# Two layers of a three-mixer decoder trunk: the up projection's three products per step as two, and the gated features on GpSimd

## The chip, the core and the metric

The kernel runs on one core of a Trainium2 chip. The metric is the device time of one execution in microseconds, as the median of the runs. The engines are TensorE (PE in the rows; its weight loads are PEld), VectorE (DVE), ScalarE (ACT), GpSimd (POOL) and SyncE (SP), which issues most transfers. SBUF is the working memory, PSUM (banks of 128 x 512 float32) takes TensorE's results; GpSimd has no access to PSUM.

## What is computed

Two layers over 256 positions of 1024 features, float32. The part that the change touches is the feed-forward half of each layer, cut from the reference:

```python
h = rmsnorm(x, norm_ffn)
u = causal_depthwise_conv(h @ w_up, conv_w, conv_b)     # w_up: 1024 x 5632, 3 taps
u_a, u_v = jnp.split(u, 2, axis=-1)                     # 2816 features each
return x + (jax.nn.silu(u_a) * u_v) @ w_down            # w_down: 2816 x 1024
```

Ahead of it each layer has one combined input projection, three attention-like mixers and their merge. The output is a final rmsnorm.

## The kernel before

**Products in two parts.** Float32 numbers are cut into a high part (a copy rounded to TensorE's 32-bit format F32R) and a low part (the number minus the high part). A product is then three: high weights x high activations, high x low, low x high (`three`, L347). Activations lie with the position as the free axis, 256 columns, with the two halves of the positions interleaved by `turns` when TensorE reads them.

**Weights.** `weights` (L260) loads a piece of 1 MB by a transfer on SP into one of 4 `raw` tiles, ScalarE writes the high part `whi` (L271), VectorE the low part `wlo` (L272): in this text a "split". One piece makes two pairs of 128x1024, and there are 6 buffers of each (`wp`), so TensorE must be done with a pair before the pair six later can be written. A pair serves 8 k steps of one 128-wide block of output features, called a tile below: 24 products.

**Up projection** (L733 to L782). Eleven passes `i`, each with two pieces (`a` = 0 for the features that go through silu, 1 for the others) of two tiles `f`: four tiles a pass. A tile's result has 256 columns in a PSUM tile (`at` for a = 0, `mm` for a = 1, `at` for both in the last pass; four banks each). `conv` (L719) does the convolution: ScalarE's Identity with the last tap as scale and the bias (L727), then two steps of VectorE, `scalar_tensor_tensor` shifted by one and by two positions (L728, L729). In the first pass the row scale of the norm isn't known yet, and VectorE multiplies it in (L724). Then silu on ScalarE (L768), the product with the other half on VectorE (L770), and a split of the result into `gT`, again by L271 and L272. All small tiles come from a pool `quarter` of 8 buffers.

**Down projection.** In layer 0 (L783 to L795) each of 8 output blocks runs over all k = 0 to 21 before the next begins, 22 x 3 products of 256 columns; `grow` adds the result to x. In layer 1 (L798 on) four sums run side by side over k = 0 to 17, and over k = 18 to 21 at the end, with products of 512 columns. There passes 4 to 7 of the up projection also transpose a piece of x, and ScalarE copies it (L782).

**Order.** TensorE's program order is as written. A scheduler places the instructions of VectorE, ScalarE and GpSimd in their queues when the program is built; each engine then takes its queue in order and waits at its head. GpSimd has little to do before: the power of the norm (L309, L821) and one multiply of 128x512 in `scaled` (L336).

Of the kernel before, what the change touches and what calls it, by code (L numbers as in the profile page):

```python
# [9 lines left out]
F32 = mybir.dt.float32  # L10
F32R = mybir.dt.float32r
BF = mybir.dt.bfloat16
AF = mybir.ActivationFunctionType
OP = mybir.AluOpType
# [4 lines left out]
S = 256  # L19
# [98 lines left out]
def trunk(ctx: ExitStack, tc: tile.TileContext, x, wpack, vecs, sinks, gain_out, rope, masks, fc, out):  # L118
    nc = tc.nc
# [11 lines left out]
    f3 = lambda a, n=S: a.rearrange("p (k n) -> p k n", n=n)  # L131

    def mm(n=512):
        t = pm.tile([128, 512], F32, name="mm", tag="mm")
        return t
# [13 lines left out]
    def parts(mov, k):  # L149

        return mov[k // 2][:, k % 2] if isinstance(mov, list) else mov[:, k]

    def turns(v):

        return (v if len(v.shape) == 3 else v.rearrange("p (h i) -> p h i", h=2)).rearrange("p h i -> p i h")
# [5 lines left out]
    def halves(v):  # L161
        return v.rearrange("p (h i) -> p h i", h=2) if len(v.shape) == 2 else v.rearrange("p a (h i) -> p a h i", h=2)
# [5 lines left out]
    def quarter():  # L168
        return tp.tile([128, S], F32, name="quarter", tag="quarter", bufs=8)
# [6 lines left out]
    def matmul(out, lhsT, rhs, **kw):  # L176
        n = 1
        for k in rhs.shape[1:]:
            n *= k
        clock[0] += n / 2400 * (4 if lhsT.dtype == F32 else 1)  # L180
        return nc.tensor.matmul(out, lhsT, rhs, **kw)  # L181
# [9 lines left out]
    def resume(task):  # L191
        try:
            task[0] = next(task[1]) + clock[0]
        except StopIteration as e:
            tasks.remove(task)
            task[1] = None

    def tick():
        for task in list(tasks):
            if clock[0] >= task[0]:  # L200
                resume(task)
                break
# [11 lines left out]
    first = [rawp.tile([128, 2048], F32, name="raw", tag="raw") for _ in range(2)]  # L214
# [45 lines left out]
    def weights(l, i, n=1024):  # L260

        r = rawp.tile([128, 2048], F32, name="raw", tag="raw")
        nc.sync.dma_start(r, wpack[l, i])
        w = [new_cut() for _ in range(2)]
        for a in range(0, 2048, n):
            hi, lo = (q[:, a % 1024 : a % 1024 + n] for q in w[a // 1024])
            split(hi, lo, r[:, a : a + n])
        return lambda a, n: [q[:, a % 1024 : a % 1024 + n] for q in w[a // 1024]]

    def split(hi, lo, src):  # L270
        a = nc.scalar.activation(hi, src, AF.Copy)  # L271
        return a, nc.vector.tensor_tensor(lo, src, hi.bitcast(F32), OP.subtract)  # L272
# [74 lines left out]
    def three(ps, lh, ll, rh, rl, first, last):  # L347
        ps, rh, rl = ps.rearrange("p (i h) -> p i h", h=2), turns(rh), turns(rl)
        matmul(ps, lh, rh, start=first, stop=False)
        matmul(ps, lh, rl, start=False, stop=False)  # L350
        matmul(ps, ll, rh, start=False, stop=last)
        tick()

    def gemm_a(l, i, act, n=512):

        ws = [weights(l, i)] + ([weights(l, i + 1)] if n == 512 else [])
        per = 2048 // n
        ps = [mm(), mm()]
        for t, k in [(t, k) for k in range(8) for t in range(2)]:
            wh, wl = ws[k // per](k % per * n, n)  # L360
            three(ps[t][:, :n], act[:, k, t, 0, :], act[:, k, t, 1, :], wh, wl, k == 0, k == 7)
        return ps

    def gemm_b(w, f, mov, ps, nk=8, ks=None):

        for k in ks or range(nk):
            wh, wl = w((f * nk + k) * 128, 128)
            v = parts(mov, k)
            three(ps, wh, wl, v[:, :, 0, :], v[:, :, 1, :], k == 0, k == nk - 1)

    def rotary(dst, ps, t, nh, kind):

# [180 lines left out]
    last = DEPTH - 1  # L553

    ctx.enter_context(tc.manual_schedule(engines={mybir.EngineType.PE}))
    for l in range(DEPTH):
        pc = 0
        vB = f3(blk(), 512)
        if l == 0:
            st = {}  # L560
            ps = [mm(), mm()]
            for k in range(KT):
# [5 lines left out]
                if k % 2 == 0:  # L568
                    wh, wl = new_cut()
# [8 lines left out]
        else:  # L578
            ps = gemm_a(l, pc, st["h"])
        h = st["h"]  # L580
# [4 lines left out]
        for n in range(2):  # L585
            d = f3(blk())
            for c in range(2):
                w = ahead if l == 0 and pc == 2 else weights(l, pc)
                pc += 1
                ps = [(at if n == 0 and c == 1 else mm)() for _ in range(2)]  # L590
# [19 lines left out]
        h = scaled(2 * l, rb)  # L610
# [32 lines left out]
        for n in range(2):  # L643
            ps = gemm_a(l, pc, h)
            pc += 2
            tr.append(spawn(rotated(qkC[n], ps, 8, 2 * n)))
        ps = gemm_a(l, pc, h)
# [6 lines left out]
        ps = gemm_a(l, pc, h)  # L654
# [4 lines left out]
        ps = gemm_a(l, pc, h, n=256)  # L659
# [10 lines left out]
        for hf in range(2):  # L670
            m, mp = blk(), [blk2() for _ in range(2)]
            for i in BRANCHES:
                sg = blk()
                for c in range(2):
                    w = weights(l, pc)
                    pc += 1
                    for f in range(2):
                        p = mm()
                        gemm_b(w, f, h, p[:, :S])
                        j = 2 * c + f  # L680
# [3 lines left out]
                w = weights(l, pc)  # L684
                pc += 1
                until("ABC"[i])
                for f in range(4):
                    p = mm()
# [14 lines left out]
        for fs in ((0, 1, 2, 3), (4, 5), (6, 7)):  # L703
            w = [weights(l, pc + i) for i in range(len(fs) // 2)]
            pc += len(w)
            ps = [mm() for _ in fs]
            for r in range(2):
                for f, p in zip(fs, ps):
                    for k in range(4 * r, 4 * r + 4):
                        wh, wl = w[(f - fs[0]) // 2]((f % 2 * 8 + k) * 128, 128)  # L710
                        v = parts(mg, k)
# [4 lines left out]
        h = st["h"]  # L716
        tn = spawn(norm_scales(st, NORM[1]))
        gT = []
        def conv(ps, a, i):  # L719
            for f in range(2):  # L720
                j, p = a * NF + 2 * i + f, ps[f]
                if i == 0:
                    q = quarter()
                    nc.vector.tensor_tensor(q, p[:, :S], rb, OP.mult)  # L724
                    p = q
                u = quarter()
                nc.scalar.activation(u, p[:, :S], AF.Identity, scale=col(l, 88 + j), bias=col(l, 132 + j))  # L727
                nc.vector.scalar_tensor_tensor(u[:, 1:S], p[:, 0 : S - 1], col(l, 44 + j), u[:, 1:S], op0=OP.mult, op1=OP.add)  # L728
                nc.vector.scalar_tensor_tensor(u[:, 2:S], p[:, 0 : S - 2], col(l, j), u[:, 2:S], op0=OP.mult, op1=OP.add)  # L729
                us.append(u)  # L730

        ahead = None
        for i in range(11):  # L733
            us, pend = [], []
            if i == 1:
                h = hs
            for a in range(2):
                w = ahead or weights(l, pc, n=1024 if i else 512)
                ahead = None
                pc += 1  # L740
                ps = [(at if a == 0 or i == 10 else mm)() for _ in range(2)]
                if i == 0 and a == 0:
                    gemm_b(w, 0, h, ps[0][:, :S], ks=range(7))
                    gemm_b(w, 1, h, ps[1][:, :S], ks=range(7))
                    for f in range(2):
                        gemm_b(w, f, h, ps[f][:, :S], ks=[7])
                    finish(tn)
                    rb = st["row"]
                    hs = scaled(2 * l + 1, rb)
                else:  # L750
                    for f in range(2):
                        gemm_b(w, f, h, ps[f][:, :S])
                if i == 0:
                    pend.append((ps, a))
                    if a == 0:
                        continue
                else:
                    pend = [(ps, a)]
                if i == 0 and a:
                    ahead = weights(l, pc)  # L760
                for ps, a in pend:
                    conv(ps, a, i)
            for f in range(2):
                k = 2 * i + f
                if k % 2 == 0:
                    gT.append(blk2())
                sa = quarter()
                last_silu = nc.scalar.activation(sa, us[f], AF.Silu)  # L768
                g = quarter()
                nc.vector.tensor_tensor(g, sa, us[2 + f], OP.mult)  # L770
                split(*(parts(gT, k)[:, :, j, :] for j in range(2)), halves(g))
            if l == last and i == 3:

                xe = np_.tile([128, 4096], F32, name="xe", tag="xg")
                xn, gB = f3(xe[:, : 2 * D], D), xe[:, 2 * D : 3 * D]
                nc.sync.dma_start(gB, bass.AP(tensor=gain_out.tensor, offset=gain_out.offset, ap=[[0, 128], [1, D]]))
            if l == last and 4 <= i < 8:
                t, c = divmod(i - 4, 2)
                p = mm()
                for j in range(4):  # L780
                    transpose(p[:, j * 128 : j * 128 + 128], xT[:, 4 * c + j, t * 128 : t * 128 + 128])
                nc.scalar.activation(xn[:, t, c * 512 : c * 512 + 512], p, AF.Copy)  # L782
        if l < last:  # L783
            st = {}
            for f in range(KT):
                p = mm()
                for k in range(NF):
                    j = f * NF + k
                    if j % 16 == 0:
                        w = weights(l, pc)  # L790
                        pc += 1
                    wh, wl = w((j % 16) * 128, 128)
                    v = parts(gT, k)
# [4 lines left out]
    ps = [[mm(), mm()] for _ in range(2)]  # L798
# [4 lines left out]
    for t, c, k in order:  # L803
        wh, wl = ws[k // 2]((k % 2) * 1024 + c * 512, 512)
# [3 lines left out]
        if c == 0:  # L808
            y = blk()
            ss = sp_.tile([128, 2], F32, name="ss", tag="ss")  # L810
            v = sp_.tile([128, 1], F32, name="v", tag="v")
# [49 lines left out]
```

## Time and profile before

| | |
|---|---|
| median of 3 runs | 838.12 us (836.96 to 838.51) |
| profiled execution | 837.95 us, span 836.2 |
| busy TensorE, VectorE, ScalarE, GpSimd | 822.5, 654.6, 536.9, 15.2 us |
| up projection of layer 0, passes 2 to 10 | 265.5 to 361.8 us of the span |

The span is what the engines show, the rest lies around it. Busy time of TensorE is modelled and overlaps itself, so the distance from one product's start to the next is the better measure of what one costs. A row of the timeline has start, length, engine, line, operation, tiles (written <- read), shapes, and in brackets the idle time before it and what ended it; rows of the same kind in succession are merged, with their count.

### The profile page before, as it was taken

Reading aid. Unit: us, or ns where it says so; the run is one execution under the profiler, and the core shown is the slowest. Engines: PE = TensorE matmul, PEld = TensorE weight load, DVE = VectorE, ACT = ScalarE, POOL = GpSimd, SP = SyncE. Lnnn points to the kernel's source line nnn. Section 1 sums busy time; section 2 is a strip of 40 time slices with the busy share of each in tenths; the row PEclk is TensorE's granted clock in tenths of the full one; section 3 lists DMA queues with packets and bytes.
Section 4 is the critical chain, followed back from the end, with each engine's and each line's share of the span. In section 5 each row is a group of like instructions: output and inputs, shape, how many; then the busy total and the mean of one; then the engine's idle time right before and its main releaser. Section 6 shows DMA issues by size and latency. Waiting matters only on the chain.

```text
span 836.2 us, 16477 instructions
## 1 busy us (share of the span) xinstructions
PE 822.5 (98%) x6710; PEld 784.4 (94%) x6710; DVE 654.6 (78%) x1225; ACT 536.9 (64%) x893; POOL 15.2 (2%) x17
## 2 busy tenths in 40 slices
PE   8899999999999999999999999999999999999996
PEld 6888899999999999999999889999999999999885
DVE  6878798776689998876658878896568899888543
ACT  7576478665568776664446766686556687666442
POOL 0100000000010000000000000000000100000000
PEclk9999999999999999999999999999999999999998
DMA  9654442555554665565655432545664467555511
GB/s 348 261 196 151 152 146 91 206 193 182 193 202 151 213 217 192 193 200 198 201 201 198 151 107 100 201 152 158 203 199 163 162 214 249 194 202 196 203 55 50
DMA packets 22635, 151.49 MB, mean 181 GB/s; under 512 B 2656, under 2 KB 3168, under 8 KB 4896
## 3 DMA queue, kind: packets, MB, share of 16 engines
q1 hardware_dynamic: 21744, 148.86, 51.7%
q8 instruction: 52, 0.85, 0.4%
q10 hardware_dynamic: 576, 0.80, 0.3%
q0 software_dynamic: 240, 0.79, 0.3%
q14 instruction: 23, 0.19, 0.1%
HBM read 149.39 MB, written 1.05 MB: 180 GB/s over the span
## 4 chain that ended last, share of the span: by engine, by line
PE 91%; issue 4%; DVE 3%; ACT 2%; POOL 1%; POOLq 0%; ACTq 0%
PE mm L181 67%; PE at L181 21%; PE at L185 2%; DVE half L343 1%; DVE wlo L272 1%; ACT whi L271 0%; POOL rn L309 0%; PE at L316 0%; DVE hs L272 0%; ACT half L457 0%; ACT half L456 0%; ACT half L455 0%; POOL gx L217 0%; PE mm L185 0%; DVE half L459 0%
## 5 line engine op out<-in xcount | busy, mean ns | idle before, releaser
L272 DVE TENSOR_TENSOR wlo<-raw,whi 128x1024 fp32r<-128x1024 f32 (+1 forms) x292 | 342.8, 1180 | 115.2 <-ACT whi L271 115.0
L271 ACT ACTIVATE whi<-raw 128x1024 fp32r<-128x1024 f32 (+1 forms) x292 | 296.4, 1022 | 190.5 <-PE mm L181 155.6
L181 PE MATMUL mm<-hs,whi 128*128 128x256 f32 x1344 | 229.1, 276 | 0.0
L181 PEld LDWEIGHTS mm<-hs,whi 128*128 128x128 f32 x1344 | 204.1, 192 | 1.0 <-issue 0.8
L181 PE MATMUL mm<-hs,wlo 128*128 128x256 f32 x672 | 184.8, 275 | 0.0
L181 PE MATMUL mm<-blk,whi 128*128 128x256 f32 x992 | 168.1, 276 | 0.0
L181 PEld LDWEIGHTS mm<-blk,whi 128*128 128x128 f32 x992 | 150.6, 192 | 0.6 <-issue 0.3
L181 PE MATMUL mm<-blk,wlo 128*128 128x256 f32 x496 | 136.4, 275 | 0.0
L181 PEld LDWEIGHTS mm<-hs,wlo 128*128 128x128 f32 x672 | 129.0, 192 | 0.0
L181 PE MATMUL at<-hs,whi 128*128 128x256 f32 x704 | 120.1, 276 | 1.5 <-DVE hs L272 1.5
L181 PEld LDWEIGHTS at<-hs,whi 128*128 128x128 f32 x704 | 107.2, 192 | 1.9 <-DVE hs L272 1.8
L181 PE MATMUL at<-hs,wlo 128*128 128x256 f32 x352 | 96.8, 275 | 0.0
L181 PEld LDWEIGHTS mm<-blk,wlo 128*128 128x128 f32 x496 | 95.2, 192 | 0.0
L181 PE MATMUL mm<-whi,hs 128*128 128x512 f32 (+1 forms) x320 | 93.3, 364 | 0.0
L181 PEld LDWEIGHTS at<-hs,wlo 128*128 128x128 f32 x352 | 67.6, 192 | 0.0
L181 PEld LDWEIGHTS mm<-whi,hs 128*128 128x128 f32 x320 | 58.4, 189 | 8.0 <-issue 0.3
L181 PE MATMUL mm<-wlo,hs 128*128 128x512 f32 (+1 forms) x160 | 57.3, 358 | 0.0
L181 PE MATMUL mm<-whi,blk 128*128 128x512 f32 x176 | 52.5, 379 | 0.0
L181 PE MATMUL mm<-xg,whi 128*128 128x256 f32 x256 | 43.3, 276 | 0.0
L181 PEld LDWEIGHTS mm<-xg,whi 128*128 128x128 f32 x256 | 39.0, 192 | 0.1
L181 PEld LDWEIGHTS mm<-whi,blk 128*128 128x128 f32 x176 | 33.3, 189 | 4.7
L523 ACT ACTIVATE blk<-blk,nm 128x128 f32<-128x128 f32 (+1 forms) x64 | 28.2, 443 | 13.4 <-DVE nm L520 13.3
(125 smaller groups left out, 1057.6 us busy)
## 6 DMA issues: line engine op xcount, KB each, us to landing
raw<-in_wpack SPq DMA_DIRECT2D x138, 1024.0 KB, 5.0
raw<-in_wpack SPq DMA_DIRECT2D x3, 512.0 KB, 8.9
gx<-in_x POOLq DMA_DIRECT2D x3, 256.0 KB, 7.3
raw<-in_wpack SPq DMA_DIRECT2D x2, 256.0 KB, 4.7
xe<-in_gain_out SPq DMA_DIRECT2D x1, 512.0 KB, 3.5
out<-blk SPq DMA_DIRECT2D x2, 256.0 KB, 2.1
out<-blk ACTq DMA_DIRECT2D x2, 256.0 KB, 2.5
mkt<-in_masks SPq DMA_DIRECT2D x1, 320.0 KB, 7.6
```

The costliest lines, as they stand in the source:

```text
L181: return nc.tensor.matmul(out, lhsT, rhs, **kw)
L185: nc.tensor.transpose(out, in_, ident)
L271: a = nc.scalar.activation(hi, src, AF.Copy)
L272: return a, nc.vector.tensor_tensor(lo, src, hi.bitcast(F32), OP.subtract)
L343: nc.vector.scalar_tensor_tensor(n[:, k], order(xT[:, 2 * c + k, :]), gain(gi, 2 * c + k), rp, op0=OP.mult, op1=OP.mult)
L523: nc.scalar.activation(e[:, i * w : i * w + w], e[:, i * w : i * w + w], AF.Exp, bias=nm[:, j : j + 1], accum_out=sm[:, j : j + 1])
```

## The change

In passes 2 to 10 (`i > 1`) of both layers the high weights meet both parts of the activations in one product of 512 columns, whose two halves of a PSUM bank are added afterwards; the low weights are added onto the first half. ScalarE copies the second half to SBUF, VectorE adds it to the first, and the convolution reads that sum. In all passes the gated product and its low part are computed by GpSimd, the product in place. Line numbers of the changed kernel are 8 to 18 higher.

```diff
+    def two(ps, lh, ll, v, first, last):
+        both = v.rearrange("p h j i -> p (j i) h")
+        matmul(f3(ps, 2), lh, both, start=first, stop=False)
+        matmul(f3(ps[:, :S], 2), ll, turns(v[:, :, 0, :]), start=False, stop=last)
+        tick()
...
             v = parts(mov, k)
-            three(ps, wh, wl, v[:, :, 0, :], v[:, :, 1, :], k == 0, k == nk - 1)
+            if ps.shape[-1] == 2 * S:
+                two(ps, wh, wl, v, k == 0, k == nk - 1)
+            else:
+                three(ps, wh, wl, v[:, :, 0, :], v[:, :, 1, :], k == 0, k == nk - 1)
...
+                elif i > 1:
+                    q = quarter()
+                    nc.scalar.activation(q, p[:, S:], AF.Copy)
+                    nc.vector.tensor_tensor(q, p[:, :S], q, OP.add)
+                    p = q
...
-                        gemm_b(w, f, h, ps[f][:, :S])
+                        gemm_b(w, f, h, ps[f] if i > 1 else ps[f][:, :S])
...
-                g = quarter()
-                nc.vector.tensor_tensor(g, sa, us[2 + f], OP.mult)
-                split(*(parts(gT, k)[:, :, j, :] for j in range(2)), halves(g))
+                g = sa
+                nc.gpsimd.tensor_tensor(g, sa, us[2 + f], OP.mult)
+                hi, lo = (parts(gT, k)[:, :, j, :] for j in range(2))
+                nc.scalar.activation(hi, halves(g), AF.Copy)
+                nc.gpsimd.tensor_tensor(lo, halves(g), hi.bitcast(F32), OP.subtract)
```

VectorE's queue in a settled pass of layer 0 before, from the gated product of one pass on (L770, then two `blk` rows for its low part; `wlo` is a split, L728 and L729 the convolution):

```order
L770 TENSOR_TENSOR quarter<-quarter 128x256
L272 TENSOR_TENSOR wlo<-raw,whi 128x1024
L272 TENSOR_TENSOR blk<-quarter,blk 128x2x128 x2
L728 SCALAR_TENSOR_TENSOR quarter<-at,vec,quarter 128x255
L729 SCALAR_TENSOR_TENSOR quarter<-at,vec,quarter 128x254
L272 TENSOR_TENSOR wlo<-raw,whi 128x1024
```

The same engine in a settled pass after (L740 is the addition of the halves, L744 and L745 the convolution):

```order
L272 TENSOR_TENSOR wlo<-raw,whi 128x1024
L744 SCALAR_TENSOR_TENSOR quarter<-quarter,vec 128x255
L740 TENSOR_TENSOR quarter<-mm,quarter 128x256
L745 SCALAR_TENSOR_TENSOR quarter<-quarter,vec 128x254
L272 TENSOR_TENSOR wlo<-raw,whi 128x1024
```

The gated product and its low part are gone from the queue, and an addition stands in each tile's stretch between the two convolution steps of the tile before; one split stands beside one tile's convolution in both.

ScalarE at the end of layer 0's up projection after (L739 copies the second half, L743 is the Identity, L784 silu, L788 the high part of the gated product, which reads what GpSimd wrote; L624 loads the table of the next layer's functions):

```order
L739 ACTIVATE quarter<-at 128x256
L271 ACTIVATE whi<-raw 128x1024
L743 ACTIVATE quarter<-quarter,vec 128x256
L739 ACTIVATE quarter<-at 128x256
L271 ACTIVATE whi<-raw 128x1024
L743 ACTIVATE quarter<-quarter,vec 128x256
L784 ACTIVATE quarter<-quarter 128x256 x2
L624 ACT_TABLE_LOAD
L788 ACTIVATE blk<-quarter 128x2x128 x2
L271 ACTIVATE whi<-raw 128x1024 x2
```

And before, at the same place (L727 the Identity, L768 silu, `blk` the high part):

```order
L727 ACTIVATE quarter<-at,vec 128x256
L271 ACTIVATE whi<-raw 128x1024
L727 ACTIVATE quarter<-at,vec 128x256
L768 ACTIVATE quarter<-quarter 128x256 x2
L271 ACTIVATE whi<-raw 128x1024
L271 ACTIVATE blk<-quarter 128x2x128 x2
L613 ACT_TABLE_LOAD
L271 ACTIVATE whi<-raw 128x1024
L285 ACTIVATE xg<-gx 128x2x128
```

A copy now stands ahead of every tile's weight split, and the last two high parts stand behind the table load and ahead of the next weight splits.

## Rows read from the trace of the kernel before

**Rows 1.** The page's first part: busy us, share of the span, instructions.

```profile
PE 822.5 (98%) x6710; PEld 784.4 (94%) x6710; DVE 654.6 (78%) x1225; ACT 536.9 (64%) x893; POOL 15.2 (2%) x17
```

**Rows 2.** Chain of waits in order of time: start us, us, what.

```profile
286.92 5.36 PE at L181 x48
...
772.40 51.82 PE mm L181 x240
```

**Rows 3.** Windows, up projection of layer 0: length; PE, PEld, DVE, ACT, POOL; clock.

```profile
274.70:285.40 10.70, 10.70 (x98) 10.70 (x97) 10.70 (x20) 7.71 (x14) 0.00 (x0) 1.00 0.65 215
...
306.80:317.50 10.70, 10.70 (x98) 10.70 (x98) 9.54 (x17) 7.32 (x13) 0.00 (x0) 1.00 0.58 194
```

**Rows 4.** Waits from 306.8 to 349.6: us in total, times, longest.

```profile
ACT whi L271 <- PE mm L181: 9.3, 8, 1.2
ACT whi L271 <- PE at L181: 4.2, 8, 0.6
```

**Rows 5.** Timeline: a split on VectorE, and the first product of pass 2.

```profile
261.06 1.22 DVE L272 TENSOR_TENSOR wlo<-raw,whi 128x1024 fp32r<-128x1024 f32 x1
...
265.31 0.39 PE L181 MATMUL at<-hs,whi 128*128 128x256 f32 x2
```

**Rows 6.** Operations on `quarter` tiles: line, engine, count; ns min/median/max; first and last start.

```profile
L768 ACT ACTIVATE quarter<-quarter x44: 399/405/422, 262.8 to 774.0; 128x256 f32<-128x256 f32 x44
L770 DVE TENSOR_TENSOR quarter<-quarter x44: 412/423/443, 264.1 to 775.9; 128x256 f32<-128x256 f32 x44
L727 ACT ACTIVATE quarter<-at,vec x44: 536/547/562, 265.6 to 773.3; 128x256 f32<-128x256 f32 x44
L728 DVE SCALAR_TENSOR_TENSOR quarter<-at,vec,quarter x44: 475/479/499, 267.7 to 774.6; 128x255 f32<-128x255 f32 x44
L695 DVE TENSOR_TENSOR quarter<-mm,blk x32: 412/417/425, 149.6 to 629.9; 128x256 f32<-128x256 f32 x32
L727 ACT ACTIVATE quarter<-quarter,vec x8: 583/600/612, 255.3 to 669.5; 128x256 f32<-128x256 f32 x8
L728 DVE SCALAR_TENSOR_TENSOR quarter<-quarter,vec x8: 477/480/484, 256.5 to 670.9; 128x255 f32<-128x255 f32 x8
```

**Rows 7.** GpSimd: groups by line (count, busy us, mean ns), and timeline.

```profile
L821 POOL TENSOR_TENSOR r<-v,mhalf 128x1 f32<-128x1 f32 x2 | 1.1, 550 | 170.6 <-DVE v L819 170.6
L852 POOL MEMSET const-bfloat16-1.0<- 128x1 bf16 x1 | 0.1, 101 | 0.0
...
29.74 1.28 POOL L336 TENSOR_TENSOR half<-gx,rb 128x512 f32<-128x512 f32 x1 [1.30 <-DVE rb L319]
...
657.62 2.33 POOL L336 TENSOR_TENSOR half<-gx,rb 128x512 f32<-128x512 f32 x1 [1.40 <-DVE rb L319]
```

**Rows 8.** Timeline of VectorE beside those two instructions.

```profile
30.37 0.41 DVE L604 SCALAR_TENSOR_TENSOR blk<-at,rb 128x256 f32<-128x256 f32 x1
...
657.36 1.22 DVE L272 TENSOR_TENSOR wlo<-raw,whi 128x1024 fp32r<-128x1024 f32 x1
658.50 1.76 DVE L343 SCALAR_TENSOR_TENSOR half<-gx,rb 128x256 f32<-128x256 f32 x1
...
662.05 0.93 DVE L343 SCALAR_TENSOR_TENSOR half<-gx,rb 128x256 f32<-128x256 f32 x2
```

**Rows 9.** End of layer 0's up projection: VectorE's timeline; the down projection's first products.

```profile
366.90 0.76 DVE L272 TENSOR_TENSOR blk<-quarter,blk 128x256 fp32r<-128x256 f32 x2
...
L181 PE MATMUL mm<-blk,whi x139: 275/275/275, 361.8 to 384.9; 128*128 128x256 f32 x139
```

**Rows 10.** Windows at the start of the program, columns as in rows 3.

```profile
24.40:28.40 4.00, 1.88 (x16) 1.69 (x16) 3.46 (x4) 0.52 (x1) 2.72 (x1) 1.00 1.01 416
...
29.75:33.16 3.41, 3.41 (x19) 3.41 (x18) 3.34 (x8) 1.43 (x2) 1.27 (x1) 0.50 1.01 423
```

**Rows 11.** ScalarE's copies of the transposed x in layer 1, columns as in rows 6.

```profile
L782 ACT ACTIVATE xe<-mm x4: 584/586/589, 708.0 to 741.4; 128x512 f32<-128x512 f32 x4
```

## The prediction

> **What bounds the kernel now.** I read the page's busy times first, then the chain of waits through the up projections, then a table of windows over that stage, and last single rows of VectorE (DVE) and GpSimd (POOL). TensorE (PE) is busy 98% of the span, VectorE 78% [rows 1]. In the up projection the chain is TensorE alone: every run of 48 products of 256 columns takes 5.36 us, so one product costs 5.36/48 = 0.1117 us and the three of one k step 0.335 us [rows 2]. I call the 8 k steps of one 128-wide block of w_up a tile: 2.68 us. One pass of the loop over `i` has four tiles, 10.72 us.
>
> VectorE is close behind. In a settled pass (306.8 to 317.5) it works 9.54 of 10.70 us, ScalarE (ACT) 7.32; at 274.7 to 285.4 VectorE is busy all the time [rows 3]. What gives it room is a lead. There are six buffers of weight halves, so the split of tile c+6 may begin when tile c is done; in the settled stretch ScalarE waits for TensorE before it can split on, 9.3 + 4.2 us in 42.8, which is the sign of a full lead [rows 4]. At the first pass that the change touches (i = 2) the lead is small: the low halves of its first tile are ready at 261.06 + 1.22 = 262.28, and TensorE uses them at 265.31, 3.0 us later [rows 5].
>
> **The change, part by part.** TensorE: 9 passes x 4 tiles x 8 k steps x 2 layers = 576 steps lose one of three products and get the same columns in two. 512 columns cost 51.82/240 = 0.2159 us in the down projection of layer 1 [rows 2]. A step becomes 0.2159 + 0.1117 = 0.3276 instead of 0.3350: 7.4 ns less, 4.2 us in all, a tile 2.62 us, a pass 10.48. The upper end of the cost is no gain (the pair as long as three products), the lower one no overhead left (768 columns at 0.2159/512 = 0.3239, 6.4 us less). I take 4.2, since the row with 512 columns has the same 32-bit operands read with the same turn.
> The rows show 5 ns of a 256-column product beyond its share at 2.4 GHz (256/2.4 = 106.7 ns), and 2.6 ns of a 512-column one (213.3). The Trainium skill, TensorE: Matmul & The Clock Gate, section "Wait — 56ns, not 53.3ns?", has one fixed cost of about 2.5 ns for every product, whatever its width; by that rule the merge would give only 576 x 2.5 ns = 1.4 us (an estimate) where the rows give 4.2.
>
> VectorE: a pass loses two multiplies and two subtractions of 128x256 (0.42 each) and gets four additions with one input in PSUM; the nearest row, L695, takes 0.417. Its two convolution steps read an SBUF tile in place of PSUM, 0.48 either way [rows 6]. So its own work stays 9.54 a pass.
> ScalarE: four copies more, between 0.405 (SBUF, L768) and 0.547 (PSUM, L727), and the Identity from SBUF 0.600 in place of 0.547 [rows 6]: 1.8 to 2.4 a pass on 7.32, so 9.1 to 9.7 of 10.48. That hides behind TensorE as long as ScalarE doesn't wait.
> Buffers: 10 `quarter` tiles a pass in place of 8, in 8 buffers; a copy then waits for a tile of the pass before, which costs nothing while GpSimd is done within a pass. PSUM banks come free earlier, at the addition. The weight DMAs keep their order on SP.
>
> GpSimd is where I see the cost: four instructions a pass, each with SBUF inputs. The trace has one such operation in this program, L336, 128x512: 1.28 us alone [rows 7]. At 657.62 it finds VectorE in a split of two SBUF inputs (657.36 to 658.58) and takes 2.33: it waited 0.96 and then ran about as long as alone. VectorE's next instruction, also of two SBUF inputs, is issued at 658.50 and takes 1.76, where the two of its kind at 662.05 take 0.93 together. It ended 0.31 after GpSimd, so it stood still for 1.3 us. At 29.74 to 31.02 VectorE's product of PSUM and one SBUF tile beside L336 took 0.41 as ever [rows 8]. So either engine waits for the other's whole instruction when VectorE reads two SBUF tiles. In the new passes that is every split (four, 1.2) and every convolution step (eight, 0.48); only the additions can run beside GpSimd.
>
> Length of one 128x256 instruction on GpSimd: half of L336 is 0.64; with the 0.55 that a one-column instruction takes as a fixed part it is 0.55 + 0.73/2 = 0.91; with the 0.10 of a MEMSET, 0.10 + 1.18/2 = 0.69 [rows 7]. I take 0.7, since a one-column power is another operation.
> The Trainium skill, GPSIMD Engine Reference, section 3.1, measures 4497 ns for an fp32 addition of 2048 columns; a line through that and L336 gives 0.74 for 256 (an estimate), by which the result would be some 3 us later than mine.
>
> A pass then asks of VectorE 9.54 + 4 x 0.7 = 12.3, less what stands beside additions (0.34 from start to start, as the two rows of 0.42 that take 0.76 together [rows 9]; at most four, I take two): 11.7, bounds 10.7 (0.64 and all four) and 13.2 (0.91 and none). TensorE needs 10.48. A tile costs VectorE 2.93 and TensorE 2.62: the lead shrinks by 0.3 a tile. ScalarE follows, since its copy of the gated half waits for GpSimd's multiply in the middle of its queue, ahead of the next weight halves.
>
> Where it comes out. The passes 0 and 1 have no addition and lose 1.7 us of VectorE work, against 2.8 us of holds, so the lead still grows from 3 to some 5 us until the first addition. Then 5/0.3 = 17 tiles use it up, and of the 36 tiles about 8 are left in which TensorE waits 0.3: 2.5 us a layer. The saving of 2.1 us a layer is gone there.
> The end of layer 0 is worse. The convolution of tile c stands in VectorE's row beside the split of tile c+6. Before, the last gated halves are written at 366.90 + 0.76 = 367.7, with TensorE in the down projection since 361.8 [rows 9]; its first block asks for them at k = 20 and 21, 6.7 us in, so they come about in time. With no lead left, VectorE has five tiles to go when the down projection starts: 5 x 2.93 = 14.6, then multiply, copy and subtractions, 2.5 to 4 with the holds. 14.6 + 4 - 6.7 = 12 us of standing TensorE (8 to 16). After such a pause the granted clock falls: in the one place of the trace where it did, TensorE had worked 1.88 of 4.00 us, and ran the 3.41 us from 29.75 at 0.50 of full speed, 1.2 GHz [rows 10], so 1.7 us are lost.
> In layer 1 the down projection goes through all k before the last four, so late gated halves wait for nobody, but six tiles of splits still come 2.93 apart where TensorE takes 12 x 0.2159 = 2.59: 2.0, and ScalarE's four copies of 0.59 (L782) [rows 11] cost part of theirs, 0.5.
>
> Sum: -4.2 + 2 x 2.5 + 12 + 1.7 + 2.5 = +17. On the profiled execution, 837.95 (span 836.2 and 1.75 around it; the median is 838.12), that is 855 us.
>
> **Rivals.**
> 1. GpSimd doesn't hold VectorE (the wait of 1.3 us being an accident of that place). VectorE stays at 9.54 of 10.48, only the last chain is about 1 us longer: 837.95 - 4.2 + 1 = 834.8, faster. The place is the same pass; it decides from where a hold costs VectorE less than (10.48 - 9.54)/4 = 0.23 us. Against it stand both directions of the wait [rows 8].
> 2. The holds are there, but short and mostly beside additions: 10.7 a pass, 2.69 a tile. The lead stays near 3 us, no waits in the passes, and the end of layer 0 costs about 4 and the clock 1.7: 837.95 - 4.2 + 5.7 = 839.5. For it: VectorE has 0.4 to 0.5 us gaps in its settled row; against it, in the first passes it has none.
> 3. GpSimd is slower (0.91), so that ScalarE, waiting on its multiply, and VectorE both fall back: 13.2 a pass, excess 0.68 a tile. 22 tiles of waiting a layer are 2 x 15, the end 13, clock 1.7, layer 1's rest 4: 837.95 - 4.2 + 48.7 = 882.
> 4. The merge gives nothing (pair = three products), the rest as forecast: 859.
>
> **Chances.** Forecast (with rival 4, whose time lies in its range) 0.74, rival 1 0.10, rival 2 0.08, rival 3 0.08. Own range of the forecast 846 to 868. Leaving out rival 1, half of rival 2 and the far part of rival 3 gives 840 to 873. A measurement here can tell about 0.2% (1.7 us) from no change: faster 0.10, the same 0.04 (half of rival 2), slower 0.86.
>
> **What would show it.** Products of 512 and 256 columns 0.2159 and 0.1117 apart in the new passes; GpSimd rows of 0.7, longer behind a split; some VectorE rows of 0.48 and 1.2 lengthened by about 0.7; VectorE filled in the late passes; no more waits of ScalarE for TensorE there; and one long idle time of TensorE some 7 us into layer 0's down projection, waiting for a gated half, with the clock at half after it. If that idle time is missing, the term of 12 is wrong; if VectorE's rows keep their lengths beside GpSimd, the whole forecast falls to rival 1.

## The result

| | before | after |
|---|---|---|
| median | 838.12 us (836.23 to 838.51, 5 runs) | 850.85 us (848.53 to 851.12, 5 runs) |
| span of the profiled execution | 836.2 | 849.3 |
| layer 0, passes 2 to 10 | 96.5 | 96.3 |
| layer 0, down projection | 56.3 | 70.0 |
| layer 1, passes 2 to 10 | 98.2 | 99.0 |

The ratio is 1.0158, 95% interval 1.0144 to 1.0171: slower, by 12.7 us; 855 was forecast. The stages run from TensorE's first use of the low weights of one tile to that of another (in the down projection from its first tile to its last), worked out from the timeline. The stretch ahead of them, where TensorE's products are the same, is 1.4 us shorter in this trace of after; over all traces shown here it differs by up to 3.7 us, so spans are compared by stage. The trace of before has 3.41 us at half the clock near the start [rows 10], and that of after has a granted clock of 1.00 there, from 29.75 to 33.16.

The page's busy times of after, beside those of before [rows 1]:

```profile
PE 821.8 (97%) x6134; PEld 766.2 (90%) x6134; DVE 672.0 (79%) x1209; ACT 557.4 (66%) x965; POOL 103.6 (12%) x105
```

576 products fewer, and TensorE's busy time is nearly the same: the columns are as many as before, and part of the products ran at a slower clock, as seen below. The chain of waits of after (start us, us, what), at the start of the passes and near their end:

```profile
264.05 5.24 PE at L181 x32
...
361.27 0.48 DVE quarter L744
...
362.48 1.14 DVE wlo L272
363.61 0.87 DVE quarter L744
...
364.74 1.02 DVE quarter L745
...
365.82 1.65 POOL quarter L786
...
368.56 0.48 DVE quarter L745
```

Two tiles take 5.24 us where they took 5.36 [rows 2]: the merge pays 0.06 a tile, as worked out, 2.2 us a layer. That is 7.5 ns a step, not the one fixed cost of about 2.5 ns that the Trainium skill (TensorE: Matmul & The Clock Gate, "Wait — 56ns, not 53.3ns?") would save by a product less. But from 335 on the chain has all but left TensorE (one run of 2.90 us is left in it) and goes through VectorE, ScalarE and GpSimd; the piece from 346.0 to 368.56 is two passes, 11.28 us each, beside 10.48 of TensorE.

Windows of after (columns as in [rows 3]):

```profile
307.50:318.00 10.50, 10.50 (x66) 9.66 (x66) 9.90 (x16) 8.01 (x15) 3.36 (x5) 1.00 0.52 178
339.00:349.50 10.50, 10.50 (x66) 9.62 (x65) 9.90 (x16) 7.69 (x17) 4.15 (x4) 1.00 0.57 200
349.50:360.00 10.50, 9.14 (x54) 7.92 (x53) 9.90 (x16) 7.74 (x15) 4.13 (x4) 1.00 0.62 202
360.00:370.50 10.50, 7.52 (x62) 6.93 (x60) 9.90 (x15) 8.03 (x16) 4.13 (x4) 0.97 0.54 182
370.50:381.00 10.50, 3.70 (x15) 3.41 (x16) 7.30 (x12) 6.96 (x12) 3.11 (x4) 0.50 0.38 123
```

TensorE is full until about 350, gets holes in the last pass, and stands in the down projection. VectorE is not quite full in them: 9.90 of 10.50. The lead of the low halves, from the end of a tile's split to TensorE's first use of it, is 3.3 us at the first tile of pass 2, 1.1 three tiles on, rises to 5.7 at 290 and falls to 0.1 at 348; before, it rose to 11.1 by 311 and stayed. The 1.1 comes from GpSimd's part in passes 0 and 1, as e1 and e2 below have 5.9 and 1.2 at that tile. There ScalarE waits 1.60 and 1.67 us for GpSimd, and splits grow, this one beside GpSimd's multiply:

```profile
263.56 1.74 DVE L272 TENSOR_TENSOR wlo<-raw,whi 128x1024 fp32r<-128x1024 f32 x1
```

Where TensorE stood, in its timeline (idle time and its end in brackets):

```profile
367.97 0.38 PE L181 MATMUL mm<-blk,whi 128*128 128x256 f32 x1 [1.31 <-ACT blk L788]
368.77 0.38 PE L181 MATMUL mm<-blk,whi 128*128 128x256 f32 x1 [0.43 <-POOL blk L789]
376.46 0.58 PE L181 MATMUL mm<-blk,whi 128*128 128x256 f32 x1 [7.20 <-ACT blk L788]
377.88 0.58 PE L181 MATMUL mm<-blk,whi 128*128 128x256 f32 x1 [0.84 <-POOL blk L789]
```

9.8 us for gated halves of the last two passes, k = 19 and 20. Products then run at half the clock until 383.4, 5.5 us, so about 3 us more are lost: 12.8 of the 13.7 that the down projection grew.

Beside GpSimd's rows, the groups by line (count, ns min/median/max; first and last start; form):

```profile
L786 POOL TENSOR_TENSOR quarter<-quarter x44: 723/1038/1712, 261.8 to 801.8; 128x256 f32<-128x256 f32 x44
L789 POOL TENSOR_TENSOR blk<-quarter,blk x44: 722/734/1715, 263.5 to 803.0; 128x256 fp32r<-128x256 f32 x44
L744 DVE SCALAR_TENSOR_TENSOR quarter<-quarter,vec x80: 471/482/964, 255.1 to 799.7; 128x255 f32<-128x255 f32 x80
L745 DVE SCALAR_TENSOR_TENSOR quarter<-quarter,vec x80: 467/476/1011, 255.8 to 800.7; 128x254 f32<-128x254 f32 x80
L740 DVE TENSOR_TENSOR quarter<-at,quarter x40: 409/419/425, 274.0 to 797.9; 128x256 f32<-128x256 f32 x40
```

GpSimd alone takes 0.72, up to 1.71 behind a split; the convolution steps, of two SBUF tiles, reach twice their length; the addition, of PSUM and one SBUF tile, never grows. That is the hold (either engine waiting for the other's instruction) on which the forecast was built. One place in a pass (timeline, ordered by engine):

```profile
320.49 1.21 DVE L272 TENSOR_TENSOR wlo<-raw,whi 128x1024 fp32r<-128x1024 f32 x1
321.62 0.94 DVE L744 SCALAR_TENSOR_TENSOR quarter<-quarter,vec 128x255 f32<-128x255 f32 x1
323.04 0.42 DVE L740 TENSOR_TENSOR quarter<-at,quarter 128x256 f32<-128x256 f32 x1 [0.47 <-ACT quarter L739]
...
322.32 0.42 ACT L788 ACTIVATE blk<-quarter 128x256 fp32r<-128x256 f32 x1 [1.41 <-POOL quarter L786]
322.64 0.37 ACT L739 ACTIVATE quarter<-at 128x256 f32<-128x256 f32 x1
...
320.64 1.65 POOL L786 TENSOR_TENSOR quarter<-quarter 128x256 f32<-128x256 f32 x1 [0.36 <-DVE quarter L745]
```

GpSimd's multiply is issued during a split and takes 1.65; ScalarE waits 1.41 for it at the head of its queue; the copy L739 stands behind that, so VectorE's addition waits 0.47. The window of that one pass:

```profile
318.36:329.64 11.28, 11.28 (x71) 10.36 (x70) 10.67 (x18) 8.48 (x17) 4.14 (x5) 1.00 0.54 187
```

VectorE is busy 10.67 of 11.28. Three convolution steps of 0.94 to 1.00 are 1.45 longer than alone, so its own work is 9.22; 0.61 is idle, 0.47 of it the wait shown.

### The profile page after: what moved, and what is told of

Read it like the earlier page. It is cut to its first block, busy times and chain, and to the rows that moved or that the text cites. A ratio compares the mean times of both kernels' runs of the same rounds, so it can differ in the third digit from the quotient of the medians.

```text
span 849.3 us, 15525 instructions
## 1 busy us (share of the span) xinstructions
PE 821.8 (97%) x6134; PEld 766.2 (90%) x6134; DVE 672.0 (79%) x1209; ACT 557.4 (66%) x965; POOL 103.6 (12%) x105
## 4 chain that ended last, share of the span: by engine, by line
PE 74%; DVE 12%; issue 6%; ACT 4%; POOL 3%; POOLq 0%; DVEq 0%; ACTq 0%
PE mm L181 59%; PE at L181 12%; DVE wlo L272 4%; DVE quarter L744 3%; DVE quarter L745 2%; POOL quarter L786 2%; PE at L185 2%; ACT whi L271 1%; DVE half L343 1%; DVE quarter L740 1%; ACT quarter L743 1%; ACT quarter L739 1%; ACT blk L788 0%; DVE hs L272 0%; POOL rn L309 0%
## 5 line engine op out<-in xcount | busy, mean ns | idle before, releaser
L181 PE MATMUL mm<-hs,whi 128*128 128x256 f32 (+1 forms) x1088 | 227.5, 302 | 1.8 <-DVE quarter L740 1.8
L181 PEld LDWEIGHTS mm<-hs,whi 128*128 128x128 f32 x1088 | 174.8, 191 | 9.9 <-DVE quarter L740 2.1
L181 PE MATMUL mm<-blk,whi 128*128 128x256 f32 x992 | 171.8, 279 | 9.8 <-ACT blk L788 8.5
L181 PE MATMUL at<-hs,whi 128*128 128x512 f32 (+1 forms) x384 | 118.2, 367 | 3.2 <-DVE quarter L740 1.8
L181 PEld LDWEIGHTS mm<-blk,wlo 128*128 128x128 f32 x496 | 96.5, 195 | 0.0
L181 PEld LDWEIGHTS at<-hs,whi 128*128 128x128 f32 x384 | 70.4, 189 | 12.7 <-DVE quarter L740 2.6
L786 POOL TENSOR_TENSOR quarter<-quarter 128x256 f32<-128x256 f32 x44 | 52.1, 1184 | 154.0 <-ACT quarter L784 135.6
L309 POOL TENSOR_TENSOR rn<-var,mhalf 128x2 f32<-128x2 f32 x4 | 4.8, 1212 | 522.2 <-DVE var L307 522.2
L743 ACT ACTIVATE quarter<-quarter,vec 128x256 f32<-128x256 f32 x80 | 47.6, 595 | 30.3 <-DVE quarter L740 26.4
L744 DVE SCALAR_TENSOR_TENSOR quarter<-quarter,vec 128x255 f32<-128x255 f32 x80 | 52.6, 657 | 2.1 <-ACT quarter L743 2.1
```

The costliest lines, as they stand in the source:

```text
L309: nc.gpsimd.tensor_tensor(rn, v, mhalf.to_broadcast([128, 2]), OP.pow)
L786: nc.gpsimd.tensor_tensor(g, sa, us[2 + f], OP.mult)
```

## The experiments

All in one table; the differences are those of the stages above, in us against before. "Up" is passes 2 to 10, "down" layer 0's down projection. Lead is that of the last tile of layer 0's up projection. The median is that of the run, the ratio against before in the same session.

| run | median | ratio, 95% interval | up 0 | down 0 | up 1 | lead |
|---|---|---|---|---|---|---|
| after | 850.85 | 1.0158 (1.0144 to 1.0171) | -0.2 | +13.7 | +0.8 | 2.1 |
| e2_gpsimd_only | 838.07 | 1.0003 (0.9993 to 1.0013) | 0.0 | 0.0 | 0.0 | 10.9 |
| e1_merge_only | 863.77 | 1.0319 (1.0300 to 1.0338) | +8.1 | +9.0 | +10.9 | 19.8 |
| e5_no_reads | 832.68 | 0.9945 (0.9929 to 0.9962) | -2.2 | +0.8 | -2.2 | 10.6 |
| e9_no_add | 837.72 | 0.9998 (0.9986 to 1.0011) | -2.2 | +5.0 | -2.2 | 5.4 |
| e6_merge_near | 851.37 | 1.0158 (1.0141 to 1.0174) | +1.0 | +12.2 | -0.7 | 3.7 |
| e7_after_near | 863.43 | 1.0313 (1.0296 to 1.0330) | +4.1 | +14.7 | +3.8 | 0.1 |
| e3_late_k | 845.71 | 1.0097 (1.0080 to 1.0113) | -0.2 | +6.9 | +1.6 | 2.1 |
| e4_merge_late_k | 857.38 | 1.0240 (1.0220 to 1.0261) | +6.5 | +2.2 | +9.7 | 18.4 |
| e10_late_merge_late_k | 840.14 | 1.0030 (1.0020 to 1.0040) | -1.2 | +4.8 | -1.2 | 2.5 |
| e11_late_merge | 846.79 | 1.0111 (1.0095 to 1.0126) | -1.2 | +11.0 | -1.2 | 2.5 |
| e12_mid_merge_late_k | 847.77 | 1.0126 (1.0112 to 1.0140) | +1.1 | +7.3 | +1.4 | 0.1 |
| e13_by_the_lead | 834.77 | 0.9967 (0.9955 to 0.9978) | -0.7 | 0.0 | -1.2 | 4.2 |

**One part alone.** e1 has the merge and computes the gated features on VectorE as before; e2 has the three products of before and the gated features on GpSimd.

```diff
 e1, from after:
-                g = sa
-                nc.gpsimd.tensor_tensor(g, sa, us[2 + f], OP.mult)
...
+                g = quarter()
+                nc.vector.tensor_tensor(g, sa, us[2 + f], OP.mult)
+                split(*(parts(gT, k)[:, :, j, :] for j in range(2)), halves(g))
 e2, from after (`two` goes too):
-                elif i > 1:
-                    q = quarter()
-                    nc.scalar.activation(q, p[:, S:], AF.Copy)
-                    nc.vector.tensor_tensor(q, p[:, :S], q, OP.add)
-                    p = q
...
-                        gemm_b(w, f, h, ps[f] if i > 1 else ps[f][:, :S])
+                        gemm_b(w, f, h, ps[f][:, :S])
```

> The two-product form with copies and additions, the gated features on VectorE and ScalarE as before; nothing on GpSimd. Theory A (VectorE's queue is too full, and the end of layer 0 pays): VectorE 9.54 + 4 x 0.34 = 10.9 us a pass against 10.48 of TensorE, the lead falls to 1 to 2 us by the last pass, TensorE stands about 7 us in layer 0's first down block, clock 1.7: 842 to 844 us. Rival B (all of the loss is GpSimd's holds): no standing, 834 us.

> Three products as before, no additions, only the gated product and its low part on GpSimd. Theory A with holds: VectorE gives up 4 x 0.34 and gets 4 x 0.72 of holds, about 10.9 to 11.1 us a pass against 10.72, a lead of 2 to 4 us at the end of the up projection, TensorE stands 5 to 9 us in layer 0's first down block, clock 1.7: 845 to 849 us. Rival B2 (no holds, VectorE is simply relieved): 837 to 838 us.

GpSimd alone costs no time, though not for the reason of rival B2: the holds are there, yet VectorE is busy 8.71 us of a settled pass, where it was 9.54 [rows 3], since the gated features are gone from it. Timeline of e2, and the window of one pass:

```profile
322.71 1.60 DVE L272 TENSOR_TENSOR wlo<-raw,whi 128x1024 fp32r<-128x1024 f32 x1 [1.11 <-ACT whi L271]
...
344.98:355.70 10.72, 10.72 (x99) 10.72 (x98) 8.71 (x14) 7.27 (x13) 3.58 (x5) 1.00 0.59 198
```

e1 missed both expectations. Its waits of TensorE, 255 to 400 (us in total, times, longest):

```profile
PE at L181 <- DVE quarter L740: 6.6, 3, 4.7
PE mm L181 <- ACT blk L271: 6.2, 1, 6.2
```

TensorE waits for additions to free PSUM banks while the weights are ready far ahead (lead 19.8). In VectorE's queue the convolution of a tile stands behind a split up to seven tiles further on than in before: with another mix of instructions the scheduler had chosen another order. So e1 does not measure the additions alone, and e6 was made for that.

**The hold, and the addition, taken away.** e5 replaces GpSimd's two steps by three fills, which read nothing (the gated features are constants); VectorE's queue in layer 0 is row for row that of after, in layer 1 four splits stand two rows later. e9 leaves out the addition: ScalarE copies the first half, the convolution reads the copy, and the products of high weights and low activations are left out of the sum.

```diff
 e5, from after:
-                nc.gpsimd.tensor_tensor(g, sa, us[2 + f], OP.mult)
+                nc.gpsimd.memset(us[2 + f], 0.5)
+                nc.gpsimd.memset(g, 0.5)
...
-                nc.gpsimd.tensor_tensor(lo, halves(g), hi.bitcast(F32), OP.subtract)
+                nc.gpsimd.memset(parts(gT, k).bitcast(F32), 0.5)
 e9, from after:
-                    nc.scalar.activation(q, p[:, S:], AF.Copy)
-                    nc.vector.tensor_tensor(q, p[:, :S], q, OP.add)
+                    nc.scalar.activation(q, p[:, :S], AF.Copy)
```

> The changed kernel, but GpSimd's multiply and subtraction replaced by fills of the same tiles (us and the gated tile, then both parts of gT behind ScalarE's copy), which read nothing from SBUF; the gated features are left out of the computation. VectorE's queue is the same row for row. Theory A (GpSimd's reads hold VectorE): VectorE's rows keep 0.48 and 1.2 us, 835 to 839 us. Theory D (the holds matter little; VectorE and ScalarE with copies, additions and waits on each other are what fills up): still 845 to 850 us.

> The changed kernel without VectorE's addition of the halves: ScalarE copies the first half and the convolution reads that copy, so the products of the high weights with the low activations are left out of the sum; TensorE, ScalarE and GpSimd do as much as before. Theory A/D3 (VectorE's time a pass decides: 9.54 - 1.36 + holds of 1.1 to 2.2, under 10.48): 834 to 836 us. Theory D (ScalarE's copies and its waits for GpSimd decide): 845 us or more.

Convolution and split of e5, by line as above, and a window:

```profile
L744 DVE SCALAR_TENSOR_TENSOR quarter<-quarter,vec x80: 466/479/485, 256.5 to 773.7; 128x255 f32<-128x255 f32 x80
L272 DVE TENSOR_TENSOR wlo<-raw,whi x292: 678/1224/1246, 6.2 to 811.4; 128x1024 fp32r<-128x1024 f32 x134, 128x512 fp32r<-128x512 f32 x12
...
307.50:318.00 10.50, 10.50 (x66) 9.66 (x65) 9.37 (x17) 8.41 (x17) 2.24 (x6) 1.00 0.58 200
```

Without reads of GpSimd no row grows, the lead goes to 10.9, and the merge's 2.2 us a layer arrive whole: theory D falls (832.68 is below the 835 to 839 of theory A). That GpSimd's reads and not its writes hold VectorE is what the Trainium skill says (SBUF — State Buffer, "Who interferes with whom"); these rows agree, 485 ns beside 964. The fills are also shorter (0.31 and 0.53 us), so ScalarE waits less, and the two effects aren't told apart. Without the additions (e9) the passes keep up too; but the lead stays near 5.5, the last gated halves are late by 1.7 + 0.7 us, and the window from 370.5 to 381 has a clock of 0.85: layer 0 gives 5.0 back, and 837.72 is above the 834 to 836 expected. So with the gated features off VectorE it can bear either the additions or the holds, and not both in this order of the queues.

**The order of the queues.** e6 is e1 with the splits placed behind the convolution of the pair four earlier, so that additions alone are tried in an order near that of before; e7 puts the same constraint on after.

```diff
+        def queued(p, n=1024):
+            with ExitStack() as es:
+                for q in behind.get(p - 4, ()):
+                    es.enter_context(tc.issue_after(q.ins))
+                return weights(l, pc, n=n)
...
-                w = ahead or weights(l, pc, n=1024 if i else 512)
+                w = ahead or queued(2 * i + a, 1024 if i else 512)
```

> As e1_merge_only (two products, additions, gated features on VectorE), with one thing more: the splits of a pair of tiles are queued behind the convolution of the pair four earlier, so that no convolution stands more than six tiles of splits back (in e1_merge_only up to thirteen). Theory A2 (e1's 864 came from the order of VectorE's queue, which left PSUM banks unread): VectorE 10.9 us a pass against 10.48, short standing at the end of layer 0, 836 to 843 us. Theory D2 (the additions alone overfill VectorE and ScalarE): 850 us or more.

> The changed kernel with the same ordering as e6_merge_near: the last convolutions stand behind the split five tiles on, before seven. Theory A2: the last gated halves come up to two tiles (5 us) earlier, the standing of 9.8 us shrinks: 844 to 848 us. If the lateness is from the lead alone: 851 us.

One pass of e6, its waits from 300 to 348 (L748 is the addition, L751 the Identity, L752 the convolution step), and one pass of e7:

```profile
313.80:325.40 11.60, 11.60 (x73) 10.69 (x72) 10.59 (x21) 8.46 (x17) 0.00 (x0) 1.00 0.52 177
...
ACT quarter L751 <- DVE quarter L748: 11.6, 14, 1.4
DVE quarter L752 <- ACT quarter L751: 4.8, 9, 0.7
```

```profile
334.64:346.87 12.23, 11.12 (x64) 9.62 (x64) 10.58 (x17) 8.48 (x17) 3.83 (x5) 1.00 0.48 172
```

e6 came out as theory D2 had it: with the gated features on VectorE and none of their steps on GpSimd, 851.37 us, as slow as after. VectorE's busy time of a pass is the same in after, e6 and e7 within 0.1 (10.67, 10.59, 10.58): additions with the gated features cost what additions with the holds cost. Against TensorE's 10.48 that alone would lose little. What differs is how long VectorE stands: 0.6, 1.0 and 1.65. Copy, addition, Identity, step: a tile changes engine three times between two queues that are taken in order. e7 missed both its expectations. In a settled pass a tile's convolution stands behind the split seven tiles on in after, six in e7; that with it pulled forward less other work stood between the links of that chain is the likely reason, and not shown by a run of its own.

**The end of layer 0.** e3 and e4 are after and e1 with the first two blocks of layer 0's down projection going through k = 0 to 17 of both before k = 18 to 21, which asks for the last gated halves some 6 us later.

```diff
-            for f in range(KT):
...
+            dorder = [(f, k) for f in range(2) for k in range(NF - 4)]
+            dorder += [(f, k) for f in range(2) for k in range(NF - 4, NF)]
+            dorder += [(f, k) for f in range(2, KT) for k in range(NF)]
```

> The changed kernel with one thing more: in layer 0's down projection the first two output blocks go through k = 0 to 17 first and take k = 18 to 21 afterwards, so the late gated halves are asked for 18 steps (6.0 us) later. Theory A (the standing TensorE of 9.8 us is the wait for the last gated halves): 6 us less standing, the clock's 1.7 perhaps too: 843 to 845 us. Rival C (TensorE would wait for weights or PSUM banks there anyway): 851 us.

> Two-product form, gated features on VectorE and ScalarE as before, and layer 0's first two down blocks with the late k last. Theory A: most of the 7 us of standing in e1_merge_only is hidden by 6 us of other products and the clock doesn't fall: 834 to 837 us, under the kernel before. Rival B (no standing in e1_merge_only to begin with): 834 us here and there.

Waits and window of e3:

```profile
PE mm L181 <- ACT blk L788: 2.6, 1, 2.6
PE mm L181 <- POOL blk L789: 1.0, 1, 1.0
...
370.50:381.00 10.50, 6.74 (x44) 6.16 (x44) 8.17 (x13) 8.88 (x14) 3.13 (x4) 0.87 0.41 126
```

9.8 us of standing become 3.6, and the down projection's excess falls from 13.7 to 6.9: with the 12.8 read from the trace of after, the wait and the clock behind it are most of that stage's loss. The median, 845.71, is just above the 843 to 845 expected. e4 is 6.4 us below e1, and far from its expectation: in its passes 6.5 and 9.7 us are lost, much as in e1's (8.1 and 10.9).

**Merging only where there is a lead.** The order of k of e3 in e10, e12 and e13, that of after in e11; the merge in passes 6 to 10 (e10, e11), 4 to 10 (e12), and in 5 to 7 of layer 0 and 6 to 10 of layer 1 (e13). For e13:

```diff
-                elif i > 1:
+                elif (5 <= i < 8 if l < last else i > 5):
```

> The kernel after with the merge in passes 6 to 10 only (passes 2 to 5 keep three products and no addition; gated features on GpSimd throughout), and the first two down blocks of layer 0 taking k = 0 to 17 of both before k = 18 to 21. Theory A (a merged pass takes 11.25 us of the vector engines and uses up lead; nothing is lost until the lead is gone): unmerged passes with the gated features on GpSimd raise the lead by about 0.35 us a tile, so it stands at some 8 us at the first merged tile; five merged passes use 5 x (11.25 - 10.48) = 3.9 of it, TensorE never waits in the passes, and the last gated halves come late by some 2 us less than in the kernel after, which the other order of k hides. Gain 5 x 4 x 8 x 2 x 7.4 ns = 2.4 us on 838: 835.7, between 834.5 and 837. Theory B (a merged pass costs about what its vector work is over that of TensorE wherever it stands): 838 - 2.4 + 2 x 3.9 = 843, between 841 and 846.

> The same merge in passes 6 to 10 only, but with the down projection of layer 0 in its written order. By theory A the lead left at the end is 4 to 5 us in place of 0.1, so two of the four tiles that VectorE had left when the down projection began are gone, and the last gated halves are asked for with a wait of 0 to 4 us (9.8 in the kernel after): 836 to 840. By theory B: 843 to 850. If this one is over 2 us above the kernel with the other order of k, the end of layer 0 costs time even with a lead.

> The merge in passes 4 to 10, with the other order of k in layer 0. Theory A: the lead is about 6 us at the first merged tile, seven passes use 7 x 0.77 = 5.4 of it, which just suffices: gain 7 x 4 x 8 x 2 x 7.4 ns = 3.3 us, less up to 2 us at the end of layer 0: 835 to 838. Theory B: 838 - 3.3 + 2 x 5.4 = 845.

All three were slower than theory A had it: e10 lies between the two theories' ranges, e11 in that of B, e12 above both. A's price of a pass was wrong. e10, one pass (window, then timeline):

```profile
339.23:351.36 12.13, 12.13 (x77) 11.15 (x76) 10.09 (x17) 8.27 (x17) 3.93 (x5) 1.00 0.50 172
...
339.23 0.69 DVE L744 SCALAR_TENSOR_TENSOR quarter<-quarter,vec 128x255 f32<-128x255 f32 x1 [1.23 <-ACT quarter L743]
344.89 0.48 DVE L744 SCALAR_TENSOR_TENSOR quarter<-quarter,vec 128x255 f32<-128x255 f32 x1 [0.74 <-ACT quarter L743]
...
351.36 0.69 DVE L744 SCALAR_TENSOR_TENSOR quarter<-quarter,vec 128x255 f32<-128x255 f32 x1 [1.23 <-ACT quarter L743]
...
344.19 0.60 ACT L743 ACTIVATE quarter<-quarter,vec 128x256 f32<-128x256 f32 x1 [2.08 <-DVE quarter L740]
350.42 0.42 ACT L788 ACTIVATE blk<-quarter 128x256 fp32r<-128x256 f32 x1 [1.79 <-POOL quarter L786]
```

The pass takes 12.13 (from 339.23 to the row of the same kind at 351.36): 0.69 of longer rows, 1.97 of waiting for ScalarE. Ahead of the 0.74 ScalarE had waited 2.08 for VectorE's addition, ahead of the 1.23 it had waited 1.79 for GpSimd's multiply. VectorE is busy 10.09, less than TensorE's 10.48, so its work alone doesn't make this pass too long: the waiting does. A merged pass so uses 1.65 us of the lead, not 0.77. That nothing is lost in the passes while lead is left held, against theory B: in e10 and e11 TensorE doesn't wait in the passes and both layers gain 1.2 there; in e12, with two passes more, the lead is at 0.1 and the gain gone. What e10 loses is at the end of layer 0 (two waits of 1.0 us, a clock of 0.84 in the window from 370 to 380.5), 4.8 us; in the written order it is 11.0 (e11).

> The merge where the lead of the weight halves pays for it: in passes 5, 6 and 7 of layer 0 (7.5 us of lead at the first merged tile, about 1.6 a pass used, three unmerged passes behind them to win it back) and in passes 6 to 10 of layer 1 (where the runs before had 9.6 us at the first merged tile and 0.4 at the last); gated features on GpSimd throughout, and the other order of k at the start of layer 0's down projection. Theory A (the merge is worth 0.236 us a pass on TensorE and costs nothing while lead is left): 8 x 0.236 = 1.9 us below the kernel before, no wait of TensorE for gated halves at the end of layer 0: 835.5 to 837 on 838.1, a ratio near 0.998. Theory B (the vector work of merged passes costs time even with a lead): 840 or more. If it is 838 to 839, the order of k itself or the end of layer 0 takes the 1.9 us back.

e13 has the price right: in layer 0 three merged passes and three unmerged ones behind them, in layer 1 the five that the lead bears (8.9 us at the first merged tile, 3.2 at the last). Its chain (start us, us, what):

```profile
292.44 5.36 PE mm L181 x48
297.80 5.24 PE at L181 x32
...
324.00 5.24 PE mm L181 x32
329.24 5.36 PE at L181 x48
...
717.39 5.24 PE at L181 x32
...
760.18 10.48 PE at L181 x64
```

TensorE alone again through both up projections, 0.12 us shorter for every two merged tiles, 1.9 for the 16 pairs of tiles, and 1.9 by the stages; no wait of TensorE is listed from 262 to 400. 834.77 us beside 838.26 of before in the same session, 0.22 to 0.45% less: faster than both kernels. The medians differ by 3.5, the lowest times by 2.1 (834.33 and 836.39), so what goes beyond 1.9 is not put down to the edit.

## Why the prediction was right, step by step

- **The merge, -2.1 a layer:** right; -2.2 in the passes of both e5 and e9, where nothing there takes it back. Rival 4 is out.
- **GpSimd's 0.7:** 0.72 alone. Rival 3 (0.91) is out.
- **The hold:** right as a mechanism, so rival 1 is out: without the reads (e5) the kernel is 18 us faster than after, 14.8 of them in layer 0, where VectorE's queue is the same. Its size was too large: 1.45 us in the pass worked out above, not the 2.8 less 0.7 assumed, and 0.4 in e2's (the one split of 1.60). No split of after's pass grew; three convolution steps did. Nor is the hold needed for a loss of this size, as e6 shows: what fills VectorE is the additions together with either the holds or the gated features.
- **A pass of 11.7:** measured 11.28, but made up otherwise, so that it came near is partly luck. VectorE's work is 9.22 where 9.54 stood, and with the holds 10.67, little over TensorE's 10.48; 0.61 is VectorE waiting for ScalarE. VectorE filled in the late passes, which was to be seen, did not come. The prediction said that ScalarE follows and gave it no price. This is the step that the sum lacked: by busy time alone the pass is the 10.7 of rival 2, whose 839.5 had no such waiting in it. That it is a term of its own e6 and e7 show, with the same busy time and 1.0 and 1.65 of it, and e10 above all, whose pass of 12.13 has only 10.09 of work.
- **The lead, from 3 to some 5 until the first addition, then 0.3 a tile:** it fell to 1.1 first, reached 5.7 in pass 4, and then fell by 0.2 a tile (11.28 less 10.48 in a pass).
- **Waits in the passes, +2.5 a layer:** 1.9 to 2.0 in layer 0 (-0.2 against -2.1 or -2.2), but 2.5 doesn't follow from the prediction's own figures: 17 tiles of 36 leave 19, not 8, and 19 x 0.3 is 5.7 us a layer, which makes the sum +23 and the time 861. That 2.5 came near is luck: the lead lasted longer than 17 tiles, until the last pass. Over both layers 3.6 us of TensorE's waits are for a bank that L740 hadn't read yet, and not for weights as I had it.
- **Standing 12 and clock 1.7:** 9.8 and about 3; the down projection grew by 13.7, where 13.7 stood in the sum. The two errors cancel, which is luck. e3 shows the place: asked for later, 6.8 of it go.
- **Layer 1, net +2.9:** +0.8 in the passes, which is 3.0 of waits for the 2.5 of the sum, and 0.4 after them for 2.5. The late splits and ScalarE's copies of x, priced at 2.5, cost nearly nothing.

The sum had +17, the medians differ by 12.7, the spans of the two traces by 13.2, or 14.6 without the shorter start of after's. The forecast's case was the one that came; its excess over the measurement is mostly layer 1's.

Not foreseen: the order in the queues is not a fixed frame. The same parts of the change, in other orders, took 11.28 (after, the convolution behind the split seven tiles on), 12.13 (e10) and 12.23 us (e7) a pass (both six). How much of the waiting between the engines would remain in the best order is left open.

## What to carry to other kernels

A saving on the bound engine that is paid for on engines close behind it should be spent only where these have a lead, and the lead should be counted tile by tile: how much one merged pass uses, how much a plain one wins back, and how much the consumer at the end needs. The busy share doesn't show the price when two engines pass a tile back and forth (VectorE was busy 10.09 of 12.13 us in one pass that was too slow and 10.67 of 11.28 in another); measure the pass from one row to the next of its kind. After any edit, look where the scheduler put the untouched instructions before judging the edit by its time.

## What the runs showed of the hardware

- GpSimd with two SBUF inputs of 128x256 takes 0.72 us alone and up to 1.71 when issued behind a VectorE split; a fill of the same size 0.31, holding nobody.
- A wait of TensorE can cost more than its length, and need not. In e10 two waits of 1.0 us each come before a granted clock of 0.84 over the window from 370 to 380.5; in after products ran at half the clock for 5.5 us behind a pause of 7.2. Of two waits of the same length at the same place of layer 1, one (e3, 1.85 us until 742.61) was followed by 3.4 us at half the clock and the other (after, 1.83 us until 749.56) by none; layer 1's passes are 1.6 us longer than before in e3 and 0.8 in after. Windows of e3 and of after:

```profile
743.46:746.88 3.42, 3.42 (x12) 2.87 (x11) 3.04 (x7) 2.20 (x6) 0.73 (x1) 0.50 0.74 271
...
750.00:753.50 3.50, 3.50 (x25) 3.27 (x24) 3.12 (x6) 2.38 (x7) 0.66 (x1) 1.00 0.79 274
```
